# Row maxima that skip NaN: from two engines and fixed 4 MB loads to three engines, seven-row loads and a store for each group of rows

## The chip, the cores and the metric

The kernel runs on one core of a Trainium2 chip. The metric is the device time of one execution in microseconds. Before the change its median is 1297.36 us over 10 runs, from 1297.21 to 1297.71.

## The reference

```python
batch, seq, dim = 32, 2048, 2048
x = np.random.randn(batch, seq, dim).astype(np.float32)
mask = np.random.rand(batch, seq, dim) < 0.1
x[mask] = np.nan
...
return np.nanmax(x, axis=axis).astype(np.float32)      # axis = -1
```

There are 32 x 2048 = 65,536 rows of 2048 float32 numbers, 537 MB in all, and one maximum is wanted for each row. A tenth of the numbers are NaN and must be ignored. A row of NaN alone gives NaN.

## The kernel before

The rows are spread over the 128 partitions of the core's memory, so each partition handles 512 rows, or 1,048,576 numbers. The main loop (line 49 on) runs 128 times. Each round takes 512 rows, four for each partition, as one block of 4 MB.

- SyncE issues the load of the block into `xt` (line 51). The pool `io` has three such buffers of 32 KB per partition, so up to three loads are under way or in use.
- ScalarE (line 53) reads the bits as int32, which keeps positive numbers in order, and computes the square of a shifted and scaled value into the float `kt`. The shift is chosen so that the largest number of a row comes out smallest, and a NaN, which lies on the other side of the shift, comes out larger than any of them. The pool `keys` has two buffers of 32 KB per partition.
- VectorE (line 60) takes the minimum of `kt` over each row into `acc`, which keeps all 512 results of a partition until the end.

A buffer `xt` is free again when ScalarE has read it; a buffer `kt` when VectorE has.

After the loop the keys are turned back into numbers. ScalarE takes a square root (line 70), two rounds of Newton's method sharpen it on VectorE (lines 73 to 79), ScalarE undoes shift and scale (line 81), VectorE converts to integer bits (line 89). Since the results of one partition are not neighbours in the output, 64 block transposes of 32 x 32 put them in order (line 100), and one store of 256 KB writes all of them (line 104).

Each engine works through its own queue in the order of the program, and waits on semaphores for its inputs and for buffers. All loads and the store are issued from SyncE's queue, named SP or SPq in the profile. The framework places the waits; there is no hand-written order and no planner. GpSimd does nothing but set four constants.

Of the kernel before, what the change touches and what calls it, by code (L numbers as in the profile page):

```python
# [1 line left out]

# [4 lines left out]


@with_exitstack  # L10
def kernel(
    ctx: ExitStack,
    tc: tile.TileContext,
    x: bass.AP,
    axis: bass.AP,
    out: bass.AP,
):
    nc = tc.nc
    P = nc.NUM_PARTITIONS
    f32 = mybir.dt.float32  # L20
    i32 = mybir.dt.int32

    nd = len(x.shape)
    assert axis in (-1, nd - 1), axis
    D = x.shape[-1]

    x_bits = x.bitcast(i32).flatten_outer_dims()
    R = x_bits.shape[0]
    C = 4
    assert R % (P * C) == 0  # L30
    M = R // (P * C)
    x_ck = x_bits.rearrange("(m p c) d -> m p c d", p=P, c=C)

    out_flat = out.flatten_outer_dims().rearrange("r c -> (r c)")
    out_pn = out_flat.rearrange("(q s) -> q s", q=P)

    CG = float(0x50000000)
    SCALE = 2.0**-31
    BIAS = -CG * SCALE

    io = ctx.enter_context(tc.tile_pool(name="io", bufs=3))
    keys = ctx.enter_context(tc.tile_pool(name="keys", bufs=2))
    sing = ctx.enter_context(tc.tile_pool(name="sing", bufs=1))

    bias_t = sing.tile([P, 1], f32)
    nc.vector.memset(bias_t, BIAS)  # L46
    acc = sing.tile([P, M, C], f32)

    for m in range(M):
        xt = io.tile([P, C, D], i32)  # L50
        nc.sync.dma_start(out=xt, in_=x_ck[m])  # L51
        kt = keys.tile([P, C, D], f32)
        nc.scalar.activation(  # L53
            out=kt,
            in_=xt,
            func=mybir.ActivationFunctionType.Square,
            bias=bias_t,
            scale=SCALE,
        )
        nc.vector.tensor_reduce(  # L60
            out=acc[:, m, :],
            in_=kt,
            axis=mybir.AxisListType.X,
            op=mybir.AluOpType.min,
        )

    NQ = M * C
    accf = acc.rearrange("p m c -> p (m c)")
    y = sing.tile([P, NQ], f32)
    nc.scalar.activation(y, accf, mybir.ActivationFunctionType.Sqrt)  # L70
    for it in range(2):
        r = sing.tile([P, NQ], f32, tag=f"nr{it}")
        nc.vector.reciprocal(r, y)  # L73
        t = sing.tile([P, NQ], f32, tag=f"nt{it}")
        nc.vector.tensor_mul(t, accf, r)  # L75
        s = sing.tile([P, NQ], f32, tag=f"ns{it}")
        nc.vector.tensor_add(s, t, y)  # L77
        y = sing.tile([P, NQ], f32, tag=f"ny{it}")
        nc.vector.tensor_scalar_mul(y, s, 0.5)  # L79
    gf = sing.tile([P, NQ], f32)  # L80
    nc.scalar.activation(  # L81
        gf,
        y,
        mybir.ActivationFunctionType.Copy,
        bias=CG,
        scale=-(2.0**31),
    )
    gb = sing.tile([P, NQ], i32)
    nc.vector.tensor_copy(out=gb, in_=gf)  # L89

    B = 32
    assert M % P == 0
    U = M // P
    fin = sing.tile([P, U, P, C], i32)
    g4 = gb.rearrange("p (q u c) -> p q u c", u=U, c=C)
    for u in range(U):
        for j in range(C):
            for bi in range(P // B):
                for bj in range(P // B):
                    nc.vector.transpose(  # L100
                        out=fin[bi * B : (bi + 1) * B, u, bj * B : (bj + 1) * B, j],
                        in_=g4[bj * B : (bj + 1) * B, bi * B : (bi + 1) * B, u, j],
                    )
    nc.sync.dma_start(
        out=out_pn, in_=fin.rearrange("q u p c -> q (u p c)").bitcast(f32)
    )


# [1 line left out]
_INS = ['x', 'axis']  # L110
_OUTS = [((32, 2048), 'float32')]
#: Inputs that are plain numbers.
_NUMBERS = {'axis': -1}


# [26 lines left out]
```

## Time and profile before

| what | us |
|---|---|
| median of 10 runs | 1297.36 |
| the profiled execution, its own time | 1297.55 |
| its span from first to last recorded instruction | 1295.8 |
| VectorE busy | 1138.4 |
| ScalarE busy | 915.4 |
| GpSimd busy | 0.2 |
| one load, median from issue to landing | 21.9 |

Two lines of the page tell how the bytes were moved:

```profile
DMA packets 18582, 537.19 MB, mean 415 GB/s; under 512 B 2064, under 2 KB 2064, under 8 KB 2192
HBM read 536.87 MB, written 0.26 MB: 415 GB/s over the span
```

In a group of instructions, the profile gives the line and engine, the operation, its output and input tiles with partitions and elements, the count, then the busy time, the mean of one in ns, and the idle time just before these instructions with what ended it. In the slices, each digit stands for a fortieth of the span and gives the busy share in tenths. Busy time of an engine that overlaps a slower one does not lengthen the kernel, so the page must be read together with the waits and the timeline.

### The profile page before, as it was taken

Reading aid. Unit: us, or ns where it says so; the run is one execution under the profiler, and the core shown is the slowest. Engines: PE = TensorE matmul, PEld = TensorE weight load, DVE = VectorE, ACT = ScalarE, POOL = GpSimd, SP = SyncE. Lnnn points to the kernel's source line nnn. Section 1 sums busy time; section 2 is a strip of 40 time slices with the busy share of each in tenths; the row PEclk is TensorE's granted clock in tenths of the full one; section 3 lists DMA queues with packets and bytes.
Section 4 is the critical chain, followed back from the end, with each engine's and each line's share of the span. In section 5 each row is a group of like instructions: output and inputs, shape, how many; then the busy total and the mean of one; then the engine's idle time right before and its main releaser. Section 6 shows DMA issues by size and latency. Waiting matters only on the chain.

```text
span 1295.8 us, 761 instructions
## 1 busy us (share of the span) xinstructions
DVE 1138.4 (88%) x202; ACT 915.4 (71%) x132; POOL 0.2 (0%) x4
## 2 busy tenths in 40 slices
DVE  3998998998988988998998998998898898998998
ACT  4776776776776776776776776776776777777760
POOL 0000000000000000000000000000000000000000
DMA  9999999999999999999999999999999999999940
GB/s 405 436 433 426 436 433 426 436 435 424 436 434 425 434 436 427 433 435 430 430 435 431 430 434 433 428 434 433 427 435 433 426 436 435 425 435 435 427 194 8
DMA packets 18582, 537.19 MB, mean 415 GB/s; under 512 B 2064, under 2 KB 2064, under 8 KB 2192
## 3 DMA queue, kind: packets, MB, share of 16 engines
q1 hardware_dynamic: 18576, 537.14, 96.4%
q14 instruction: 6, 0.05, 0.0%
HBM read 536.87 MB, written 0.26 MB: 415 GB/s over the span
## 4 chain that ended last, share of the span: by engine, by line
DMA 73%; ACT 24%; DVE 3%; issue 0%; ACTq 0%; SPq 0%; DVEq 0%
DMA xt<-in_x_dram 73%; ACT kt L53 24%; DVE fin L100 1%; DVE acc L60 1%; DVE r L73 1%; DVE s L77 0%; DVE t L75 0%; DVE y L79 0%; ACTq L53 0%; ACT gf L81 0%; ACT y L70 0%; DVE gb L89 0%; SPq L51 0%; DVEq L137 0%
## 5 line engine op out<-in xcount | busy, mean ns | idle before, releaser
L60 DVE TENSOR_REDUCE acc<-kt 128x4 f32<-128x8192 f32 x128 | 1111.7, 8686 | 151.2 <-ACT kt L53 151.2
L53 ACT ACTIVATE kt<-xt,bias_t 128x8192 f32<-128x8192 int32 x128 | 911.6, 7122 | 328.8 <-DMA xt<-in_x_dram 328.8
L100 DVE STREAM_TRANSPOSE fin<-gb 32x32 int32<-32x32 int32 x64 | 15.9, 248 | 0.9
L53 ACT ACT_TABLE_LOAD x1 | 1.3, 1283 | 13.4 <-DMA xt<-in_x_dram 13.4
L81 ACT ACTIVATE gf<-y 128x512 f32<-128x512 f32 x1 | 0.6, 629 | 10.6 <-DVE y L79 10.6
L73 DVE RECIPROCAL r<-y 128x512 f32<-128x512 f32 x2 | 6.7, 3353 | 0.7 <-ACT y L70 0.7
L70 ACT ACTIVATE y<-acc 128x512 f32<-128x512 f32 x1 | 0.6, 629 | 7.5 <-DVE acc L60 7.5
L77 DVE TENSOR_TENSOR s<-t,y 128x512 f32<-128x512 f32 x2 | 1.4, 693 | 0.1
L75 DVE TENSOR_TENSOR t<-acc,r 128x512 f32<-128x512 f32 x2 | 1.4, 692 | 0.1
L70 ACT ACT_TABLE_LOAD x1 | 1.3, 1283 | 0.0
L89 DVE CAST gb<-gf 128x512 int32<-128x512 f32 x1 | 0.4, 427 | 0.7 <-ACT gf L81 0.7
L79 DVE TENSOR_SCALAR y<-s 128x512 f32<-128x512 f32 x2 | 0.9, 428 | 0.1
L46 DVE MEMSET bias_t<- 128x1 f32 x1 | 0.1, 59 | 0.8 <-PEq L123 0.8
L123 POOL MEMSET const-bfloat16-1.0<- 128x1 bf16 x1 | 0.1, 103 | 0.0
L123 POOL MEMSET const-uint8-127<- 128x1 uint8 x1 | 0.1, 102 | 0.0
L123 POOL MEMSET const-float32-0.0<- 128x1 f32 x1 | 0.1, 100 | 0.2 <-issue 0.2
L123 POOL MEMSET const-float32-1.0<- 128x1 f32 x1 | 0.1, 99 | 0.0
## 6 DMA issues: line engine op xcount, KB each, us to landing
xt<-in_x_dram SPq DMA_DIRECT2D x128, 4096.0 KB, 21.9
out_dram<-fin SPq DMA_DIRECT2D x1, 256.0 KB, 2.0
```

Of the source, the lines that this page charges most:

```text
L46: nc.vector.memset(bias_t, BIAS)
L53: nc.scalar.activation(out=kt, in_=xt, func=mybir.ActivationFunctionType.Square, bias=bias_t, scale=SCALE,)
L60: nc.vector.tensor_reduce(out=acc[:, m, :], in_=kt, axis=mybir.AxisListType.X, op=mybir.AluOpType.min,)
L70: nc.scalar.activation(y, accf, mybir.ActivationFunctionType.Sqrt)
L73: nc.vector.reciprocal(r, y)
L75: nc.vector.tensor_mul(t, accf, r)
L77: nc.vector.tensor_add(s, t, y)
L79: nc.vector.tensor_scalar_mul(y, s, 0.5)
L81: nc.scalar.activation(gf, y, mybir.ActivationFunctionType.Copy, bias=CG, scale=-(2.0**31),)
L89: nc.vector.tensor_copy(out=gb, in_=gf)
L100: nc.vector.transpose(out=fin[bi * B : (bi + 1) * B, u, bj * B : (bj + 1) * B, j], in_=g4[bj * B : (bj + 1) * B, bi * B : (bi + 1) * B, u, j],
L123: nc = _bacc.Bacc("TRN2", target_bir_lowering=False, num_devices=1)
```

## The change

The loop is rebuilt around three engines that work on the upper 16 bits of each number. Taken as a signed integer `h`, the upper half of a positive number is at most `TOP` = 0x7F7F for finite ones, and the NaN in the data has `h` = 0x7FC0.

- ScalarE (line 96 of the changed kernel, as all line numbers in this section) reads every second 16-bit word of `xt` and computes a parametric ReLU of `EDGE - h`. For a number this is `TOP - h` after rounding. For NaN the argument is negative and the slope `alpha` makes it 32768. The keys are written as packed 16-bit integers into `kt`.
- GpSimd (line 104), unused so far, computes `TOP - key` and writes it back over the upper halves in `xt`, in place. A number gets its own upper half back and is again the float that it was. A NaN gets the upper half 0xFF7F, which makes it a very large negative float.
- VectorE (line 112) takes the float maximum of each row straight from `xt`.

A buffer `xt` is now free only when VectorE has reduced its last piece. It holds seven rows per partition, 56 KB, and there are three; `kt` has two buffers of four rows of 16-bit keys, 16 KB.

The table `GROUPS` sets the sizes. Its outer entries are 14 groups of rows, then buffers, then loads, then pieces. Most buffers have one load of seven rows, worked on as a piece of four and one of three (`[[4, 3]]`). There are 11 groups of six such buffers and one of four. The last two groups are cut finer: 4 and 3; 3, 2 and 2; 2, 1+1, 1, 1 and 1; and one single row in a buffer of its own. This makes 81 loads and 152 pieces. Within a group each partition takes neighbouring rows, so its results are neighbours in the output and no transpose is needed.

At the end of a group two small operations follow on VectorE. `none` (line 120) marks rows whose maximum is the replaced NaN, and `fin` (line 129) turns these into NaN by an OR of the bits. The store of a group is issued from SyncE's queue after the first load of the group two further on (line 92); the last two stores come at the end (line 134). Square root, Newton steps and transposes are gone. A one-element activation (line 72) loads ScalarE's table at the start.

```diff
+FULL = [[4, 3]]
+GROUPS = [[FULL] * 6] * 11 + [
+    [FULL] * 4,
+    [[[4], [3]], [[3], [2], [2]]],
+    [[[2], [1, 1], [1], [1], [1]], [[1]]],
+]
+WIDE = 7
+PIECE = 4
+TOP = 0x7F7F
+NAN = 0x7FC0
+LOW = -129
+EDGE = TOP + 0.25
+NONE = -255.0 * 2.0**120
...
     io = ctx.enter_context(tc.tile_pool(name="io", bufs=3))
-    keys = ctx.enter_context(tc.tile_pool(name="keys", bufs=2))
+    mid = ctx.enter_context(tc.tile_pool(name="mid", bufs=2))
+    res = ctx.enter_context(tc.tile_pool(name="res", bufs=3))
     sing = ctx.enter_context(tc.tile_pool(name="sing", bufs=1))
+    top = sing.tile([P, 1], f32)
+    nc.vector.memset(top, EDGE)
+    warm = sing.tile([P, 1], f32)
+    nc.scalar.activation(out=warm, in_=top, func=PRELU, alpha=0.5)
...
-    for m in range(M):
-        xt = io.tile([P, C, D], i32)
-        nc.sync.dma_start(out=xt, in_=x_ck[m])
-        kt = keys.tile([P, C, D], f32)
-        nc.scalar.activation(
-            out=kt,
-            in_=xt,
-            func=mybir.ActivationFunctionType.Square,
-            bias=bias_t,
-            scale=SCALE,
...
-        nc.vector.tensor_reduce(
-            out=acc[:, m, :],
-            in_=kt,
-            axis=mybir.AxisListType.X,
-            op=mybir.AluOpType.min,
...
+    for s, g in zip(rows, GROUPS):
+        xg = xr[r0 : r0 + P * s].rearrange("(p s) d -> p (s d)", p=P)
+        og = of[r0 : r0 + P * s].rearrange("(p s) -> p s", p=P)
+        r0 += P * s
+        acc = res.tile([P, s], f32, tag="acc")
+        at = 0
+        for tl in g:
+            xt = io.tile([P, WIDE * D], i32, tag="xt")
+            base = at
+            for ld in tl:
+                c = sum(ld)
+                nc.sync.dma_start(
+                    out=xt[:, (at - base) * D : (at - base + c) * D],
+                    in_=xg[:, at * D : (at + c) * D],
+                )
+                if len(stores) > 1:
+                    nc.sync.dma_start(**stores.pop(0))
+                for c in ld:
+                    xp = xt[:, (at - base) * D : (at - base + c) * D]
+                    kt = mid.tile([P, PIECE * D], u16, tag="kt")
+                    nc.scalar.activation(
+                        out=kt[:, : c * D],
+                        in_=xp.bitcast(i16)[:, 1::2],
+                        func=PRELU,
+                        bias=top,
+                        scale=-1.0,
+                        alpha=float(TOP - LOW) / (EDGE - NAN),
+                    )
+                    nc.gpsimd.tensor_scalar(
+                        out=xp.bitcast(i16)[:, 1::2],
+                        in0=kt[:, : c * D],
+                        scalar1=-1.0,
+                        scalar2=float(TOP),
+                        op0=ALU.mult,
+                        op1=ALU.add,
+                    )
+                    nc.vector.tensor_reduce(
+                        out=acc[:, at : at + c],
+                        in_=xp.bitcast(f32).rearrange("p (c d) -> p c d", c=c),
+                        axis=mybir.AxisListType.X,
+                        op=ALU.max,
+                    )
+                    at += c
+        none = res.tile([P, s], i32, tag="none")
+        nc.vector.tensor_scalar(
+            out=none,
+            in0=acc,
+            scalar1=NONE,
+            scalar2=float(0x00C00000),
+            op0=ALU.is_equal,
+            op1=ALU.mult,
...
+        fin = res.tile([P, s], i32, tag="fin")
+        nc.vector.tensor_tensor(
+            out=fin, in0=acc.bitcast(i32), in1=none, op=ALU.bitwise_or
...
+        stores.append(dict(out=og, in_=fin))
+    for st in stores:
+        nc.sync.dma_start(**st)
```

## The prediction

> **What bounds the kernel now.** I read the engines' shares first, then the slices, the costliest groups, who waited for whom, the stretches of time, and the timeline at both ends.
>
> ```profile
> DVE 1138.4 (88%) x202; ACT 915.4 (71%) x132; POOL 0.2 (0%) x4
> DMA  9999999999999999999999999999999999999940
> q1 hardware_dynamic: 18576, 537.14, 96.4%
> L60 DVE TENSOR_REDUCE acc<-kt 128x4 f32<-128x8192 f32 x128 | 1111.7, 8686 | 151.2 <-ACT kt L53 151.2
> L53 ACT ACTIVATE kt<-xt,bias_t 128x8192 f32<-128x8192 int32 x128 | 911.6, 7122 | 328.8 <-DMA xt<-in_x_dram 328.8
> L81 ACT ACTIVATE gf<-y 128x512 f32<-128x512 f32 x1 | 0.6, 629 | 10.6 <-DVE y L79 10.6
> L77 DVE TENSOR_TENSOR s<-t,y 128x512 f32<-128x512 f32 x2 | 1.4, 693 | 0.1
> L79 DVE TENSOR_SCALAR y<-s 128x512 f32<-128x512 f32 x2 | 0.9, 428 | 0.1
> ```
>
> The fullest engine is busy 88%, but it waits for ScalarE, which waits for the loads; DMA is full in every slice until the last two. The stretches (columns: VectorE, ScalarE, GpSimd busy, clock, DMA share, GB/s) say the same:
>
> ```profile
> 600.00:1240.00 640.00, 571.55 (x67) 468.31 (x67) 0.00 (x0) 1.00 1.00 432
> 1256.00:1296.00 40.00, 34.35 (x74) 1.55 (x3) 0.00 (x0) 1.00 0.02 7
> ```
>
> So the load stream sets the time up to its end, and the last 40 us is a tail with nothing loading. The timeline gives both ends:
>
> ```profile
> 0.73 58.95 SPq L51 DMA_DIRECT2D xt<-in_x_dram  x8
> 13.36 1.28 ACT L53 ACT_TABLE_LOAD   x1 [13.36 <-DMA xt<-in_x_dram]
> 1247.87 7.12 ACT L53 ACTIVATE kt<-xt,bias_t 128x8192 f32<-128x8192 int32 x1 [2.58 <-DMA xt<-in_x_dram]
> 1276.13 16.73 DVE L100 STREAM_TRANSPOSE fin<-gb 32x32 int32<-32x32 int32 x64
> 1292.89 0.35 SPq L104 DMA_DIRECT2D out_dram<-fin  x1
> ```
>
> First landing 13.36, last 1247.87: 127 loads in 1234.5 us, 9.72 us for each 4.194 MB, or 431.5 GB/s. The first took 13.36 - 0.73 = 12.63 us, so a load has 12.63 - 9.72 = 2.91 us of latency beside its transfer. The tail from the last landing is 1295.8 - 1247.9 = 47.9 us. The profiled execution took 1297.55 us, 1.75 over its span and 0.19 over the median of 1297.36.
>
> **What the Trainium skill says.** (1) "DMA: Bandwidth & Descriptors", Specifications: the fabric ceiling is 435 GB/s. The trace agrees: 431.5 leaves 0.083 us per load to gain. (2) "GPSIMD Engine Reference", 3.1 Elementwise: a loop body of at most two operations runs at 1.03 cycles per element (0.86 ns at that page's 1.2 GHz), but the best case of a tight loop is put at 1.8 cycles (1.5 ns); 4.1 Engine selection calls one-input operations roughly line-rate. No run here shows it: GpSimd only sets constants. (3) "SBUF — State Buffer", Who interferes with whom: VectorE and GpSimd share a port pair. A `tensor_reduce` never contends, but a `tensor_scalar` in a two-port mode does, and so does an instruction with two SBUF inputs against a GpSimd one that reads SBUF; the loser blocks for the other's whole instruction. The trace shows the mode in use: TENSOR_SCALAR takes 428 ns where TENSOR_TENSOR takes 693 for the same 512 elements. It cannot show the blocking.
>
> **The change, part by part.** All prices for other sizes come from two rows each. ScalarE: (7122 - 629)/7680 = 0.845 ns per element plus 0.196 us; so 4 rows 7.12 us, 3 rows 5.39. VectorE: (8686 - 693)/7680 = 1.041 ns plus 0.16 us (both taken as streams of one element per step); 4 rows 8.69, 3 rows 6.55, 2 rows 4.43, 1 row 2.29. Reading every second 16-bit word I price as the int32 of before (the step stays 4 bytes), and max as min. The sums, with 152 pieces for 128, are ScalarE 886 + 30 = 916 us and VectorE 1092 + 24 = 1116, both under the stream. GpSimd, new: 0.86 ns plus 0.2 us assumed dispatch (0.1 from its memset row as the floor); 4 rows 7.24, 3 rows 5.48, 930 in all. I take the low figure because the operation has one input and two ALU steps, and keep 1.5 for the range.
>
> *The stream.* The bytes stay: 536.87 MB at 431.5 GB/s is 1244.2 us. There are 81 loads for 128; if the 0.083 us goes with the number of packets, 47 x 0.083 = 3.9 us is saved, if with bytes nothing: I take 2. Twelve small stores now run in the same SP queue between loads. What they store is long finished, so they hold nothing by waiting, but 128 packets of 168 bytes pass through the engines: from 0 to 1 us each (the store of before took 2.0 from issue to landing, most of it latency); I take 0.3, or 3.6 in all. Last landing: 0.73 + 2.91 + 1244.2 - 2 + 3.6 = 1249.4, if the stream never stops.
>
> *Does it stop?* A buffer was free after ScalarE (7.12 us after landing). Now it is held until the second reduction on it ends: 7.14 (ScalarE 4 rows) + 7.24 (GpSimd) + 8.70 + 6.57 (both reductions, with hand-over) = 29.7 us after landing; ScalarE's and GpSimd's 3-row pieces lie beside the first reduction. Its next load needs 2.91 + 17.01 (7/4 of 9.72). The round is 49.6 us against 3 x 17.01 = 51.0 for the three buffers' loads: 1.4 us spare. The stream holds, narrowly.
>
> *The tail.* Newton steps, table change and 64 transposes (1263.7 to 1292.9) go. But VectorE stands 29.7 us behind the landings and needs 15.3 us for every 17.0 of loading. The last buffers' pieces make it work without a gap, so the lag shrinks only by 17.0 - 15.3 to 28.0 after the 4+3 buffer, by 17.0 - 15.5 to 26.5 after 3+2+2, by 17.0 - 16.0 to 25.5 after 2+1+1+1+1+1, and to 25.4 after the last row (2.3 against 2.4). The tapered loads can't do more, since VectorE and not the landing is late. Then two small operations, 0.4, and issue and store as before (from 1292.86 to 1295.8), 2.9: a tail of 28.7. Span 1249.4 + 28.7 = 1278.1, with 1.75 around it 1279.9. The one-row load must wait for the 4+3 buffer, released 28 us after its landing; the loads of the two buffers between take 34 us, so this costs nothing.
>
> *The group ends.* `none` (TENSOR_SCALAR, 42 elements, an even number, in SBUF) and `fin` (TENSOR_TENSOR, two SBUF inputs) stand on VectorE between the last reduction of a group and the first of the next; all later reductions queue behind them. On a clock from the landing of the group's last buffer, VectorE reaches `none` at 29.7. GpSimd is then in the next buffer's 4-row piece, which runs from 17.0 + 7.1 = 24.1 to 31.4, and its 3-row piece is ready behind it (ScalarE ends that at 29.6), filling 31.4 to 36.9. Without a lock the two cost 0.4 us, inside the spare. With it, `none` waits to 31.4, which costs nothing as the next reduction needs that piece anyway; but then `fin`, or both, wait out the 3-row piece. The next reduction starts at about 37.1 instead of 31.4: 5.7 late, the buffer is released as late, and the spare 1.4 covers a part, so the stream stops for 4.3 us. VectorE regains 1.7 per buffer, so before the next group end all is as before, and it happens again. Twelve such ends, 52 us, less about 1 for the last ones, where VectorE and not the stream decides: 51.
>
> **Forecast: 1279.9 + 51 = 1331 us**, with the lock at work and GpSimd at line rate; chance 0.36. Its own range is 1318 (VectorE slips in at one group end in four) to 1360 (GpSimd at 1.0 ns, a longer wait).
>
> **Rivals.**
> - *No blocking* (0.30): the same sum without it, 1280; between 1272 (all packet savings, free stores) and 1292 (stores of 1 us). It speaks for this that two operations of some 0.2 us may slip in together between two GpSimd pieces; against it that GpSimd's next piece is always ready. This is the faster side.
> - *GpSimd a little slower* (0.17). From 1.02 ns the 1.4 us spare is used up, and each further 0.01 adds 8192 x 0.01 = 0.08 us per round of three buffers, over 25 rounds 2 us: 1296 at 1.10, 1313 at 1.18, the time of before at about 1.10. Above 1.19 its own 14336 elements outlast the 17.0 us load and it is the bound: about 1375 at 1.25. The lock comes on top, to about 1450.
> - *GpSimd at 1.5 ns or more* (0.17): 1,048,576 x 1.5 = 1573, plus 30 dispatch, 28 before its first piece and 9 after its last: 1640 and up.
> - The strided 16-bit access slowing ScalarE is a smaller chance within the third case: its 4-row piece stands in the same round and would use the same spare.
>
> **How the numbers follow.** No change means within 0.2% (2.6 us), about what can be told here. Faster: the no-blocking case, 0.30. Same: a sliver of the third, 0.03. Slower: 0.67. The range runs from 1272, the low end of the no-blocking case, to 1450, the top of the third; left out is the last case with 0.17 and some 0.03 at the edges.
>
> **What would show it.** Right: GpSimd pieces of 7.2 and 5.5 us start to start; `none` or `fin` late, with the reduction after it some 5 us late once per group; gaps in DMA once per group; the DMA share under 0.95 in the middle. Wrong: DMA share 1.00 throughout and `fin` at once (then about 1280); or GpSimd busy without gaps and all others waiting for it (then its piece time times 75 is the answer). A VectorE lag at the last landing far from 25 us makes the tail wrong.

## The result, and the profile after

The changed kernel takes 1343.36 us (median of 8 runs, 1341.24 to 1347.11) against 1297.39 for the kernel before: the ratio is 1.0356, with a 95% interval from 1.0347 to 1.0365. The forecast was 1331, slower, within 1272 to 1450. The number is near; as shown below, the mechanism that it was built on is not what costs the time in this kernel.

The page of the changed kernel first: the engines' shares, the DMA slices, the load queue and the costliest groups.

```profile
DVE 1151.5 (86%) x181; ACT 912.5 (68%) x154; POOL 1200.3 (89%) x156
DMA  9999999999999999999999999999999999999944
q1 hardware_dynamic: 13680, 537.14, 95.5%
L112 DVE TENSOR_REDUCE acc<-xt 128x4 f32<-128x8192 f32 (+3 forms) x152 | 1108.2, 7333 | 188.0 <-POOL xt L104 188.0
L96 ACT ACTIVATE kt<-xt,top 128x8192 uint16<-128x8192 int16 (+3 forms) x152 | 911.0, 6037 | 416.1 <-DMA xt<-in_x_dram 399.3
```

The slices look as full as before, since a digit of 9 stands for anything from 90%. The stretches separate the two (VectorE, ScalarE, GpSimd busy, clock, DMA share, GB/s):

```profile
100.00:600.00 500.00, 440.02 (x67) 349.27 (x57) 460.31 (x57) 1.00 0.98 412
600.00:1200.00 600.00, 522.61 (x78) 414.01 (x68) 550.99 (x68) 1.00 0.98 411
```

Before, the middle moved 432 GB/s; now it moves 411, although ScalarE still waits 399 us for loads and no engine is full. So the stream stops and starts. The groups by shape give the price of the new GpSimd operation:

```profile
L104 POOL TENSOR_SCALAR xt<-kt 128x8192 int16<-128x8192 uint16 x71 | 662.1, 9326 | 120.0 <-ACT kt L96 111.6 <-DVE acc L112 8.3
L104 POOL TENSOR_SCALAR xt<-kt 128x6144 int16<-128x6144 uint16 x72 | 508.8, 7067 | 5.7
```

That is (9326 - 7067)/2048 = 1.103 ns per element and 0.29 us fixed, against 0.86 and 0.2 in the forecast. A four-row piece takes 9.33 us where 7.24 was expected.

The chain of waits between 100 and 180 us shows one whole round of a buffer (start, length, what):

```profile
121.03 21.62 DMA xt<-in_x_dram
...
142.73 7.13 ACT kt L96
...
149.93 9.34 POOL xt L104
...
159.29 7.17 DVE acc L112
166.47 1.43 issue
167.90 6.55 DVE acc L112
...
174.47 21.61 DMA xt<-in_x_dram
```

The 1.43 us called issue are the rest of the first reduction's 8.69 us. From load to load the round takes 174.47 - 121.03 = 53.44 us, with 51.0 for three loads at the old rate. It recurs all through the kernel, not once per group: over the full buffers, the first three aside, the landings are 17.84 us apart on the mean, 53.5 for three. The 70th landing comes at 1249.7 us, where the forecast without a stop (1249.4 less 22 rows of 2.43 us) puts it at 1195.9.

At a group end, where the forecast put its 5.7 us, the timeline of VectorE and GpSimd shows this (start, length, engine, instruction):

```profile
140.04 2.32 DVE L120 TENSOR_SCALAR none<-acc 128x42 int32<-128x42 f32 x1
142.39 0.20 DVE L129 TENSOR_TENSOR fin<-acc,none 128x42 int32<-128x42 int32 x1
142.51 8.68 DVE L112 TENSOR_REDUCE acc<-xt 128x4 f32<-128x8192 f32 x1
132.99 16.53 POOL L104 TENSOR_SCALAR xt<-kt 128x8192 int16<-128x8192 uint16 x2 [1.03 <-ACT kt L96]
```

`none` takes 2.32 us instead of some 0.2: it ends when GpSimd's four-row piece, begun at 132.99, ends at about 142.3. But the next reduction needs that piece anyway. `fin` follows at once in 0.20 us, and GpSimd's pair of pieces is only 0.07 us longer than its usual 16.46. The wait is real and costs 0.2 us, not 5.7. At all eleven ends of groups of 42 rows `fin` takes 0.20 us.

### The profile page after: what moved, and what is told of

It is laid out like the page before. It is cut to its first block, busy times and chain, and to the rows that moved or that the text cites. A ratio compares the mean times of both kernels' runs of the same rounds, so it can differ in the third digit from the quotient of the medians.

```text
span 1343.5 us, 945 instructions
## 1 busy us (share of the span) xinstructions
DVE 1151.5 (86%) x181; ACT 912.5 (68%) x154; POOL 1200.3 (89%) x156
## 4 chain that ended last, share of the span: by engine, by line
DMA 38%; DVE 27%; POOL 18%; ACT 12%; issue 4%; ACTq 0%; SPq 0%; DVEq 0%; POOLq 0%
DMA xt<-in_x_dram 38%; DVE acc L112 26%; POOL xt L104 18%; ACT kt L96 12%; DVE none L120 1%; DVE fin L129 0%; ACTq L96 0%; SPq L87 0%; DVEq L112 0%; POOLq L104 0%
## 5 line engine op out<-in xcount | busy, mean ns | idle before, releaser
L104 POOL TENSOR_SCALAR xt<-kt 128x8192 int16<-128x8192 uint16 (+3 forms) x152 | 1200.1, 7895 | 131.8 <-ACT kt L96 117.1
L112 DVE TENSOR_REDUCE acc<-xt 128x4 f32<-128x8192 f32 (+3 forms) x152 | 1108.2, 7333 | 188.0 <-POOL xt L104 188.0
L96 ACT ACTIVATE kt<-xt,top 128x8192 uint16<-128x8192 int16 (+3 forms) x152 | 911.0, 6037 | 416.1 <-DMA xt<-in_x_dram 399.3
L120 DVE TENSOR_SCALAR none<-acc 128x42 int32<-128x42 f32 (+3 forms) x14 | 38.7, 2767 | 0.4
L129 DVE TENSOR_TENSOR fin<-acc,none 128x42 int32<-128x42 int32 (+3 forms) x14 | 6.1, 439 | 0.4
## 6 DMA issues: line engine op xcount, KB each, us to landing
xt<-in_x_dram SPq DMA_DIRECT2D x70, 7168.0 KB, 21.7
xt<-in_x_dram SPq DMA_DIRECT2D x2, 3072.0 KB, 16.4
out_dram<-fin SPq DMA_DIRECT2D x11, 21.0 KB, 21.7
```

Of the source, the lines that this page charges most:

```text
L96: nc.scalar.activation(out=kt[:, : c * D], in_=xp.bitcast(i16)[:, 1::2], func=PRELU, bias=top, scale=-1.0, alpha=float(TOP - LOW) / (EDGE ...
L104: nc.gpsimd.tensor_scalar(out=xp.bitcast(i16)[:, 1::2], in0=kt[:, : c * D], scalar1=-1.0, scalar2=float(TOP), op0=ALU.mult, op1=ALU.add,)
L112: nc.vector.tensor_reduce(out=acc[:, at : at + c], in_=xp.bitcast(f32).rearrange("p (c d) -> p c d", c=c), axis=mybir.AxisListType.X, op=A ...
L120: nc.vector.tensor_scalar(out=none, in0=acc, scalar1=NONE, scalar2=float(0x00C00000), op0=ALU.is_equal, op1=ALU.mult,)
L129: nc.vector.tensor_tensor(out=fin, in0=acc.bitcast(i32), in1=none, op=ALU.bitwise_or)
```

## The experiments

The theories were: the *lock* of the forecast; the *round* (three buffers' round is longer than three loads, because GpSimd is slower than priced and because of what a stop of the stream costs); and the *layout* (rows 336 KB apart, or 56 KB packets, slow the DMA by themselves). Times are medians; each ratio is to the kernel before, run on the same chip.

**Without the operations at the group ends** (`none` and `fin` dropped):

```diff
-        none = res.tile([P, s], i32, tag="none")
...
-        fin = res.tile([P, s], i32, tag="fin")
...
-        stores.append(dict(out=og, in_=fin))
+        stores.append(dict(out=og, in_=acc.bitcast(i32)))
```

> The two small operations at the end of each group of rows are left out and the plain maxima are stored, so a row of NaN alone would not come out as NaN. Lock theory (the forecast: they hold VectorE and the buffer for some 5 us at each of twelve group ends): about 51 us less than the changed kernel, near 1292. Round theory (three buffers' round of load, ScalarE, GpSimd and both reductions is longer than three loads, because a GpSimd piece of four rows takes 9.3 us; the stream stops once a round and each restart is slow): the wait of the first operation hides behind the GpSimd piece that the next reduction needs anyway, so only 0.3 us per group and the waits in the tail go: 1325 to 1341. Layout theory (rows 336 KB apart and 56 KB packets make the DMA slower by themselves): the same as the round theory.

Measured: 1331.5 us, ratio 1.0264 (1.0248 to 1.0279). 12 us go, not 51. Its last full buffer's first piece starts at 1248.23 us, against 1249.73 in the changed kernel, so only 1.5 us come from the stream and some 10 from the tail, where the scheduler put a reduction between `none` and `fin`. These lines are of the changed kernel's tail:

```profile
1291.48 5.63 DVE L120 TENSOR_SCALAR none<-acc 128x28 int32<-128x28 f32 x1
1296.97 6.54 DVE L112 TENSOR_REDUCE acc<-xt 128x3 f32<-128x6144 f32 x1
1303.44 3.29 DVE L129 TENSOR_TENSOR fin<-acc,none 128x28 int32<-128x28 int32 x1
```

Here each of them waits by itself for a GpSimd piece. For the stream of the changed kernel the lock theory falls.

**A small operation between the two** tests the step that failed: if they only slip in together, anything between them must bring the forecast's wait back.

```diff
+        mark = res.tile([P, s], f32, tag="mark")
+        nc.vector.tensor_reduce(
+            out=mark,
+            in_=none.bitcast(f32).rearrange("p (s o) -> p s o", o=1),
...
-            out=fin, in0=acc.bitcast(i32), in1=none, op=ALU.bitwise_or
+            out=fin, in0=acc.bitcast(i32), in1=mark.bitcast(i32), op=ALU.bitwise_or
```

> A small one-input reduction of 0.2 us is put between the two operations at each group end, so that they no longer follow each other at once. It copies the mask; nothing is left out. If the port lock is real and the two only slip in together between two GpSimd pieces, the second operation now waits for the whole three-row piece, 6.9 us more at each of eleven group ends, of which at most 2.6 us are caught up per buffer: 1370 to 1420. If the second operation is not subject to a lock at all: 1342 to 1350, as the changed kernel.

Measured: 1381.38 us, ratio 1.0650 (1.0633 to 1.0668), 38 us over the changed kernel. The timeline of the same place:

```profile
140.21 1.89 DVE L120 TENSOR_SCALAR none<-acc 128x42 int32<-128x42 f32 x1
142.13 0.20 DVE L129 TENSOR_REDUCE mark<-none 128x42 f32<-128x42 f32 x1
142.36 6.80 DVE L136 TENSOR_TENSOR fin<-acc,mark 128x42 int32<-128x42 int32 x1
```

During the 0.20 us of `mark`, which has one input and reduces, GpSimd starts its three-row piece, and `fin` then waits 6.8 us for its end. So the blocking that the Trainium skill states in "SBUF — State Buffer", Who interferes with whom, is there, for an instruction with two SBUF inputs too. The forecast's price for it was of the right size (the next reduction is some 6.8 us late where it had 5.7, and 38/11 = 3.5 us are lost per group end where it had 4.3); that the two neighbours would be parted was wrong.

**GpSimd's four-row piece halved:**

```diff
+                    h = 2 if c == 4 else c
...
-                        out=xp.bitcast(i16)[:, 1::2],
-                        in0=kt[:, : c * D],
+                        out=xp.bitcast(i16)[:, 1 : 2 * h * D : 2],
+                        in0=kt[:, : h * D],
...
```

> GpSimd treats only two rows of each four-row piece (4.75 instead of 9.33 us) and the reduction reads these two rows twice, so half of the four-row pieces' rows are left out of the result; loads, ScalarE's work and VectorE's work keep their size. Round theory: the round falls from 20.0 + 7.2 + 9.3 + 15.2 = 51.7 us to 47.1, below the 51.0 of three loads; the stream no longer stops, packets of 56 KB fall from 2.19 to about 2.12 us on the mean, and the whole takes 1275 to 1290. Layout theory: packets stay at 2.17 us or more and the time is 1305 to 1320. Lock theory: still some 50 us over 1280 for the group ends, 1325 to 1335.

Measured: 1280.06 us, ratio 0.9862 (0.9846 to 0.9879). Its stretches:

```profile
100.00:600.00 500.00, 456.54 (x69) 364.34 (x60) 349.89 (x60) 1.00 1.00 433
600.00:1200.00 600.00, 547.25 (x84) 440.68 (x72) 414.43 (x71) 1.00 1.00 432
```

The DMA share is 1.00 and the rate that of the kernel before; a packet of 56 KB takes 2.12 us on the mean, against 2.19 in the changed kernel. With the same layout, packets and group ends as the changed kernel, the stream runs when a buffer is released earlier.

**Contiguous blocks:**

```diff
-                    in_=xg[:, at * D : (at + c) * D],
+                    in_=xr[r0 - P * s + P * at : r0 - P * s + P * (at + c)].rearrange(
+                        "(p c) d -> p (c d)", p=P
+                    ),
```

> Each load reads one contiguous block (56 KB from one partition's rows to the next) instead of rows 336 KB apart; the rows so end up in another order in the output. Layout theory: packets go back to about 2.12 us on the mean, and the time falls to 1300 to 1315. Round theory: no change beyond 5 us, 1338 to 1348, packets still near 2.19 us since they are slow after each stop of the stream. Lock theory: no change.

Measured: 1341.63 us, ratio 1.0348 (1.0320 to 1.0375): no change, and the packets still take 2.18 us. So the distance of the rows is not the cause; that packets of 56 KB are not either was shown by the halved piece, whose stream ran with them. The layout theory falls.

**Three and four rows instead of four and three**, one line (`FULL = [[3, 4]]`):

> One size changed: the seven rows of a buffer are worked on as three and then four instead of four and then three; still one load of seven rows. Round theory: 20.0 + 5.4 + 7.1 + 9.3 + 8.7 = 50.5 us, just below the 51.0 of three loads instead of 0.7 above. If each stop of the stream brings a slow restart of some 2 us, then a change of 1.2 us per round takes away 2.4 us per round, 23 rounds, 50 to 60 us: 1285 to 1300. If only the difference of the sums counted: 16 us, about 1327. Lock theory: 1335 to 1350.

Measured: 1343.52 us, ratio 1.0355 (1.0340 to 1.0371). The round theory's figure was missed, and the time lies in the lock theory's range. The trace gives each a part. At five of the eleven ends of 42-row groups `none` waits 8.2 to 8.7 us, for almost a whole four-row piece, although the three-row piece that the next reduction needs is already done. Here that piece is the first of the two that begin at 235.77 us, and it ends at 242.84:

```profile
235.77 16.45 POOL L104 TENSOR_SCALAR xt<-kt 128x6144 int16<-128x6144 uint16 x2 [0.64 <-ACT kt L96]
243.89 8.37 DVE L120 TENSOR_SCALAR none<-acc 128x42 int32<-128x42 f32 x1
252.41 15.14 DVE L112 TENSOR_REDUCE acc<-xt 128x3 f32<-128x6144 f32 x2
```

The next buffer is then held 37.4 us. After such a group end it takes 108.2 us on the mean to the next one, after the others 105.8. So in this order of pieces the forecast's lock does cost time in the stream, some 5 x 2.4 = 12 us by this estimate. It does not explain the rest: 52 of the first 67 full buffers are held only 30.8 us (the one at 107.2 until 137.95), 1.0 less than in the changed kernel, and with the forecast's 19.9 us for a load their round would fit into 51.0. Their loads took 21.7 us. So the other term of the round, the load's own time, had to be wrong. I took issue and last landing of every full load from the traces of eight kernels (the changed kernel and the experiments with 56 KB loads other than those with more pieces or loads), and sorted them by how long before the preceding landing each was issued. The 18 loads issued over 7 us ahead are left out, and so is the first load of each kernel; "queue long empty" stands for 1.7 to 4.8 us after that landing:

```
issued before the    loads   from landing to     from issue to
landing ahead, us            landing, median     landing, median
  queue long empty     16         -                  19.6
  2.0 to 3.0           75        18.4                21.2
  3.0 to 3.5           78        18.1                21.4
  3.5 to 4.0           76        17.6                21.5
  4.0 to 4.5          112        17.2                21.4
  4.5 to 5.5           93        17.0                21.8
  5.5 to 7.0           84        16.9                23.6
```

The forecast held that 2.91 us of lead are enough, from the first load of the kernel before. Into an empty queue that is nearly so: 19.6 us for 16.9 of transfer. But a load issued 2 to 4 us ahead, while the last packets of its forerunner run, lands 0.7 to 1.5 us late, and no loss needs about 4.5 us. In the loads issued 2 to 5.5 us ahead the sixteen DMA engines land some 2 us apart (median), against 0.9 after a long empty queue and 1.2 in an undisturbed stream. An engine that ends 2 us before the last one runs empty unless the next load is issued 2 + 2.9 = 4.9 us before the landing; this estimate is near the 4.5 of the table. All this is a reading of the traces, and no experiment made the engines drift by itself; why they do stays open.

**GpSimd at the forecast's price**: three rows of the four-row piece, in two instructions of together 7.23 us.

```diff
-                    nc.gpsimd.tensor_scalar(
-                        out=xp.bitcast(i16)[:, 1::2],
-                        in0=kt[:, : c * D],
+                    for a, b in [(0, 2), (2, 3)] if c == 4 else [(0, c)]:
+                        nc.gpsimd.tensor_scalar(
+                            out=xp.bitcast(i16)[:, 2 * a * D + 1 : 2 * b * D : 2],
+                            in0=kt[:, a * D : b * D],
...
+                        rd = rd[:, 1:3, :].unsqueeze(1).to_broadcast([P, 2, 2, D])
...
```

> GpSimd treats three rows of each four-row piece, in instructions of two rows and of one (4.75 + 2.48 = 7.23 us, the price that the forecast had put on four rows), and the reduction reads the second and third row twice, so two of the four rows are left out of the result; all other work keeps its size. A buffer is then held 7.2 + 7.3 + 15.2 = 29.7 us, as forecast. If GpSimd's price was the only term mis-sized (a load takes 19.9 us as forecast, round 49.6 of 51.0), the stream runs through: 1278 to 1286. If the load's term was mis-sized too (near an empty queue a load takes about 22 us, as the landings of the kernels so far suggest: a load must be issued some 4.5 us before the landing ahead of it), the round is 51.7 and the stream still stops: 1300 to 1325.

Measured: 1288.87 us, ratio 0.9931 (0.9915 to 0.9947), between the two figures. In its profiled run the last full load lands at 1194.8 us, near the 1195.9 of the forecast, and loads are issued 4.1 us ahead, on the edge of the table. A buffer is held 29.8 us, near the forecast's 29.7, but its load takes 21.2 us instead of 19.9, and the round 51.06 instead of 49.6. At the forecast's GpSimd price the stream would have run, barely. The 2.1 us of the four-row piece pushed it over the edge, and the load's longer time near an empty queue made the fall deep.

**Two loads for each buffer**, `FULL = [[4], [3]]`: the same pieces, but the first can start when four rows are there.

> Each seven-row buffer is filled by a load of four rows and one of three instead of one load of seven; pieces, buffers and group ends as in the changed kernel, nothing left out. Round theory: the first piece can start 7.3 us earlier, the round is 2.9 + 9.7 (four rows) + 7.2 + 9.3 + 15.2 = 44.3 us, below 51.0: the stream runs through, 1275 to 1290. Lock theory: group ends cost as forecast, 1325 to 1335. Layout theory (rows 336 KB apart): 1305 to 1320.

Measured: 1277.17 us, ratio 0.9844 (0.9829 to 0.9859): faster than the kernel before, with nothing left out. Its stretches, and its row of GpSimd:

```profile
100.00:600.00 500.00, 455.30 (x69) 369.31 (x60) 480.90 (x60) 1.00 1.00 431
600.00:1200.00 600.00, 544.64 (x84) 441.80 (x71) 576.93 (x71) 1.00 1.00 431
```

```profile
L104 POOL TENSOR_SCALAR xt<-kt 128x8192 int16<-128x8192 uint16 (+3 forms) x152 | 1200.3, 7897 | 66.6 <-ACT kt L96 60.2
```

GpSimd works the same 1200 us as in the changed kernel; what has changed is the order of landing and work, with 151 loads for 81. This is the version to keep.

**Pieces of two, three and two** (`FULL = [[2, 3, 2]]`) shorten the round in another way.

> The seven-row buffers are worked on as pieces of two, three and two rows instead of four and three; nothing is left out. Round theory: 20.0 (load) + 3.7 (ScalarE 2 rows) + 4.75 + 7.07 + 4.75 (GpSimd) + 4.4 (last reduction) = 44.7 us, below 51.0, while GpSimd's own 16.7 us per buffer stays just under the 17.0 of its load: the stream runs through, and the time is 1275 to 1290, faster than the kernel before. Lock theory: the group ends still cost, with shorter GpSimd pieces 3 to 5 us each, 1310 to 1335. Layout theory: 1305 to 1320.

Measured: 1309.74 us, ratio 1.0096 (1.0080 to 1.0111), short of the round theory's figure. The chain of its page says why:

```profile
POOL 46%; ACT 22%; DVE 21%; issue 6%; DMA 5%; POOLq 0%; DVEq 0%
```

With three pieces in two key buffers, ScalarE waits for GpSimd to free a buffer and GpSimd then 0.68 us for ScalarE:

```profile
134.22 16.76 POOL L104 TENSOR_SCALAR xt<-kt 128x6144 int16<-128x6144 uint16 x3 [0.68 <-ACT kt L96]
151.66 16.74 POOL L104 TENSOR_SCALAR xt<-kt 128x6144 int16<-128x6144 uint16 x3 [0.68 <-ACT kt L96]
```

Between 134.22 and 151.66 us GpSimd takes 17.44 us per seven rows, more than the 17.0 of their load. GpSimd has become the bound, which the expectation had ruled out by 0.3 us. The time is also close to the lock theory's 1310, and `none` waits 6.5 us at every end of a 42-row group; but GpSimd's rhythm is the same across such an end (these 17.44 us) and after it (17.42), so that wait does not set the time.

**Three loads and three key buffers**, and the same **with ScalarE writing back every third middle piece**, tried to improve on the two-load kernel.

```diff
-FULL = [[4, 3]]
+FULL = [[2], [2], [3]]
...
-PIECE = 4
+PIECE = 3
...
-    mid = ctx.enter_context(tc.tile_pool(name="mid", bufs=2))
+    mid = ctx.enter_context(tc.tile_pool(name="mid", bufs=3))
...
-                if len(stores) > 1:
+                if len(stores) > 2:
```

> Each seven-row buffer is filled by loads of two, two and three rows, each worked on as one piece; three key buffers of three rows for two of four, and the store of a group waits for one group more. Nothing is left out. Round theory: the first piece is ready about 8 us earlier than with a load of four rows (3.7 + 4.8 for 7.2 + 9.3 us after its landing), so VectorE stands less far behind the landings at the end: 1266 to 1275, below the two-load kernel's 1277. Rival: GpSimd, with three dispatches per buffer (1.103 ns x 14336 + 3 x 0.29 = 16.7 of 17.0 us), becomes the bound at some hand-over, as it did with pieces of two, three and two: 1285 to 1310.

Measured: 1280.41 us, ratio 0.9869 (0.9854 to 0.9884).

```diff
...
+                    if c == 2 and len(tl) == 3 and ld is tl[1] and tile_no % 3 == 0:
+                        nc.scalar.activation(
+                            out=xp.bitcast(i16)[:, 1::2],
+                            in_=kt[:, : c * D],
+                            func=PRELU,
+                            bias=full,
+                            scale=-1.0,
+                            alpha=1.0,
+                        )
...
```

> The three-load kernel with GpSimd relieved: in every third buffer ScalarE writes the middle two-row piece back itself (3.7 us). Nothing is left out. GpSimd's work per buffer falls by 4.8/3 = 1.6 us to some 15.5 of 17.0, so it should no longer fall behind, and the end follows the last landing by about 25 us or less: 1264 to 1274, below the two-load kernel's 1277. Rival: ScalarE's added work makes it late in turn for the next piece, or VectorE's lag decides the end whatever GpSimd does: 1275 to 1285.

Measured: 1285.73 us, ratio 0.9909 (0.9892 to 0.9926). Neither kernel fell into one of its expected ranges: 1280.41 lies between 1266 to 1275 and 1285 to 1310, and 1285.73 just above the rival's 1275 to 1285. Between 100 and 1200 us the streams run at 429 GB/s, against 431 with two loads, and the last full buffer lands at 1202.7 and 1203.0 us, against 1196.9. From there to the end it takes 75.8 and 81.0 us, against 78.3. So the three-load kernel loses more in the stream (5.8 us) than it gains in the tail (2.6), and with ScalarE's help both are longer. In both, `none` waits some 6 us at every end of a 42-row group (6.30 and 6.03 at the first). What each of these causes contributes was not separated.

**Stores one group later**, alone and with two loads:

```diff
-                if len(stores) > 1:
+                if len(stores) > 2:
```

> The changed kernel with the store of a group issued one group later, so that the store of the 28-row group no longer stands in SyncE's queue ahead of the last five loads. Only the tail can change: the last loads are issued up to 20 us earlier; if GpSimd and VectorE had idled for them, 5 to 12 us less, 1331 to 1338; if these engines were behind anyway, no change, 1342 to 1345.

> The two-load kernel with the store of a group issued one group later. In its tail GpSimd and VectorE work without a gap in spite of the late loads, so no change is expected beyond 2 us: 1275 to 1278. If the late loads cost: 5 us or more less.

Measured: 1342.33 us (1.0349, 1.0325 to 1.0373) and 1277.08 us (0.9843, 0.9828 to 0.9858): no change in either. The changed kernel's last five loads do stand behind the store that waits for `fin`, and are issued at 1307 us, but VectorE, which works or waits for the port without a gap from 1282.88 us on, is too far behind to need them sooner.

## Why the forecast was near, and where it was wrong

Against the forecast's span of 1278.1 without blocking, the profiled run (1343.5) is 65.4 us longer: 53.8 until the last full landing (1249.7 for 1195.9) and 11.6 after it. The forecast put 51 on blocked group ends in the stream. That these sums are alike is chance. By the forecast's own signs it failed: GpSimd's pieces take 9.3 and 7.1 us, the reduction after a group end is 0.2 us late, and the DMA share in the middle is 0.98, not under 0.95.

- **The step that failed**: "but then `fin`, or both, wait out the 3-row piece." The two neighbours pass together between two GpSimd pieces, and the wait before them hides behind a piece that was needed anyway. Without them the stream gains 1.5 us. The forecast's own rival had named this ("may slip in together"). With pieces of three and four rows instead, the wait before them did not hide at five of eleven group ends.
- **GpSimd's price**, 0.86 ns and 0.2 us, is 1.103 ns and 0.29 us. The price per element was taken from the Trainium skill's "GPSIMD Engine Reference", 3.1 Elementwise; this operation lies between the two figures that the forecast quotes from that page (0.86 and 1.5 ns). The third case, GpSimd a little slower, was what happened. But that case put the time at 1296 with 1.10 ns. Its bound of 1.19 ns for GpSimd leaves out the two dispatches of 0.2 us per buffer, with which it is 1.16; at the measured price the two pieces take 16.4 of 17.0 us, so this changed nothing.
- **The load's term** in the round was 2.91 + 17.01 = 19.9 us; near an empty queue it measures 21.6 to 22. With the forecast's own load term and GpSimd as measured, the round is 31.8 + 19.9 = 51.7, 0.7 too long, 16 us in 23 rounds. As measured it is 53.4, 2.4 too long, 55 us. This term, not GpSimd's alone, makes the loss.
- **The tail**: group operations cost 10 us there. Without them the end comes 83.3 us after the last full buffer's landing (1331.5 - 1248.2), where the forecast says 82.2; this part was reckoned within 1.1 us.
- **Right**: loads bound the kernel before; ScalarE at the old price on 16-bit words (7122 ns for the same 8192) and VectorE at 8.69 us; and that the small stores do not hold the loads (a group later, nothing changed; what they cost by themselves was not measured). The sum without stops, 1279.9, was met by the 1280.06 of the kernel with GpSimd's piece halved, but in part by luck: there the last full landing comes 4.5 us earlier than forecast (1191.4 for 1195.9), and the tail is 4.7 us longer (86.9 for 82.2).

## What to carry to other kernels

When every buffer passes several engines before it is free, add up the hold time and the load, and compare the round with the buffers' loads. A spare of 1.4 us in 51, on paper, was none: a load must be issued some 4.5 us before its forerunner lands, here, and each stop costs more than the missing time. Let work start on part of a buffer, as the two loads do, before looking for a faster engine. And read a port lock from what stands next to the waiting instruction: a wait for a piece that the next instruction needs too is free; a wait for a later piece, as with three and four rows, is not; and one small operation in the wrong place cost 38 us.

## What the runs showed that was not expected

- GpSimd's two-step operation on 16-bit keys takes 1.103 ns per element plus 0.29 us (9326, 7067 and 2478 ns for four, three rows and one row).
- VectorE, waiting for the shared port, gets it between two queued GpSimd pieces, and a directly following second instruction gets it as well; GpSimd loses 0.07 us by that (the changed kernel, at 142.4 us). In the nine kernels where `fin` follows `none` directly, it took 0.20 us at 98 of 99 ends of 42-row groups. At the other one, with three rows of the four-row piece, GpSimd was first and `fin` took 2.42 us.
- Loads issued 2 to 3 us before the landing ahead land 18.4 us after it instead of 16.9, while a load into a long empty queue takes 19.6 us in all.
